# Down projection: chunks in the order 3, 3, 3, 3, 2, 2, and the low part of one activation in three formed by a negation and an adding DMA

## Chip, cores and metric

One core of one Trainium2 chip runs the whole program. The metric is the device time of one execution in microseconds, from the median of several runs. TensorE (PE) does the matmuls, VectorE (DVE), ScalarE (ACT) and GpSimd (POOL) the elementwise work, and SyncE (SP) issues nearly all DMAs.

## The reference, cut to what matters

One layer of a streaming encoder over 1152 tokens of width 1024: a norm, one wide input projection, three mixers (a convolution, an attention with forgetting, a gated recurrence), their gated sum through `w_o`, and a channel mixer. The change lies in the channel mixer and the final norm:

```
u = rms_norm(x, g2) @ w_up            # 1024 -> 4096
x = x + square(relu(u)) @ w_down      # 4096 -> 1024
y = rms_norm(x, final_g)
```

All is float32. The matmuls take pairs of a rounded high part (type fp32r) and a low part (value minus high part); one product is three matmuls: high by high, high by low, low by high.

## The kernel before, in words

**The channel mixer** (`back_half`, from L1393) works on transposed data: channels on 128 partitions, tokens along the free axis. Both matrix products are done by a fast 2 x 2 block scheme with 7 products in place of 8. Operands are combined before, and results after, by additions. The products are numbered 1 to 7 and run in the order of `SLOTS` (L41): 2, 6, 5, 7, then product 1 of the next run, then 4 and 3. So a run has seven slots. `go` (L1507) issues for each slot the matmuls (`mm`), then `hook(slot)`, then `after(p)`, which empties or adds the finished product. Three PSUM tiles X, Y and Z are shared by the products of a run; product 7 adds onto Y after product 6 was read from it.

**Up runs** (`URun`) are 16, u15 first and u14 last (tokens split over two runs for u15). Each leaves seven squared activations of 128x576, which SP writes to DRAM (`ad_d`).

**Down runs** (`DRun`) are grouped by chunks of the 16 inner blocks. `CHUNKS` (L38) is 2, 3, 3, 3, 3, 2. For a chunk of n blocks there are 7 n activations in SBUF and four runs, d(c)0 to d(c)3, one for each pair of output blocks; a product has 6 n matmuls of 288 columns. The last chunk has four runs with other shapes, where weights of two output blocks lie side by side (dA, dB) and the tokens are split in 384 and 192 columns (`LP`), so that the final norm of the first part can run beside the second. After each product `DRun.after` (L1816) adds it onto `xt` on DVE.

**Feeding the activations** (`feed`, L1778). `TF[0]` counts free tiles among 28 of one tag. For each free one, `feed` issues an SP load of the next activation of the list `todo` (chunk, product, block k) into the upper half of a tile (L1792). An activation may be split two hooks later, at most two in one hook: ACT casts it into the lower half (L1783), and DVE subtracts the cast from it in place (L1784, seen in the profile at its helper, L1369). Tiles come free as the last run of a chunk uses its products (`DRun.free`), and at the start as the last up run frees its inputs: the driver's `hook` (L1947) adds 2 in six of its slots, 2 in the slot before, and 14 more in d00 to d02, two at a time.

**Weights** (`Step`, L1409). A step loads four raw blocks two runs ahead, in slots 4, 5 and 6 (`load`), builds the other three by subtraction on DVE in slots 1 and 2 of the run before its own, and splits all seven into high and low parts with ACT and DVE (`prep`). In slot 1 of d20, for example, DVE must have the last raw block of d21. All engines run their instructions in program order, so a wait there holds back the additions onto `xt` behind it.

**The sums of squares** (`square`, L1867) of the final norm: ACT squares, then an addition into `ss`, whose engine is an argument with GpSimd as its default. Both calls (L1885, L1973) pass DVE. `final` multiplies `ss` by a column of ones on PE (`fst`, L1900) and spreads the result (`fsb`).

**hook_a** (L1739) runs in the first up run, over the first half of the tokens, beside the end of the second norm: slot 2 issues `N1.fin`, slot 4 `N1.spread`, which makes PE multiply by the diagonal `dg` into `rb` (L1627).

Of the kernel before, what the change touches and what calls it, by code (L numbers as in the profile page):

```python
# [12 lines left out]
ALU = mybir.AluOpType  # L13
# [21 lines left out]
PC = 576  # L35
HP = 288
NST = 16
CHUNKS = (2, 3, 3, 3, 3, 2)  # L38
LP = ((0, 384), (384, 192))
CTS = (0, 4, 1, 5, 2, 6, 3, 7)  # L40
SLOTS = (2, 6, 5, 7, 1, 4, 3)  # L41
# [72 lines left out]
def trunk(tc, I, O):  # L114
    nc = tc.nc
    PE, V, A, GP, SY = nc.tensor, nc.vector, nc.scalar, nc.gpsimd, nc.sync
# [9 lines left out]
    with pool("cn") as cn, pool("st") as st, pool("dr", DRAM) as dr, pool("tp") as tp, \  # L126
# [28 lines left out]
        def dram(name, shape, dt=F32):  # L155
            return dr.tile(shape, dt, name=name, tag=name)
# [18 lines left out]
        ad_d = dram("ad_d", [8, NST, P, PC])  # L175
# [61 lines left out]
        def T(name, dt=F32):  # L237
            return tp.tile([P, 1152], dt, tag="T", bufs=28, name=name)
# [93 lines left out]
        with pool("ps1", PSUM) as ps:  # L332
# [972 lines left out]
            while un[0] < NWIN:  # L1305
# [26 lines left out]
                elif name in ("f_c", "q_c", "o_c"):  # L1332
                    r = (i * 3 + ("f_c", "q_c", "o_c").index(name)) * P
# [3 lines left out]
                else:  # L1337
                    r = (("g_a", "g_b", "g_c").index(name) * 8 + i) * P
# [20 lines left out]
        def RT(name):  # L1359
            return qp.tile([P, 512], F32, tag="r", bufs=4, name=name)  # L1360
# [7 lines left out]
        def sub(eng, out, a, b):  # L1368
            eng.tensor_tensor(out=out, in0=a, in1=b, op=ALU.subtract)  # L1369

        def add(eng, out, a, b):
            eng.tensor_tensor(out=out, in0=a, in1=b, op=ALU.add)  # L1372
# [20 lines left out]
        def back_half(ps, ep, q2, on1):  # L1393
# [15 lines left out]
            class Step:  # L1409
# [5 lines left out]
                def raw(self, p):  # L1415
                    if p not in self.r:
                        if p in (1, 2) and self.early:
                            if p == 1:
                                self.rt = T(f"{self.name}rt")
                            self.r[p] = self.rt[:, (p - 1) * 512:p * 512]  # L1420
                        elif p in (4, 5, 6):
                            self.r[p] = q2.tile([P, 512], F32, tag="q2", bufs=3, name=f"{self.name}r{p}")
                        else:
                            self.r[p] = RT(f"{self.name}r{p}")
                    return self.r[p][:, :self.w]
# [81 lines left out]
            def go(run, nxt, hook):  # L1507
                for slot, p in enumerate(SLOTS):
                    r = nxt if p == 1 else run
                    if r is not None:  # L1510
                        r.mm(p)
                    hook(slot)
                    if r is not None:
                        r.after(p)
# [166 lines left out]
            for u in range(16):  # L1681
# [22 lines left out]
                if u >= 2:  # L1704
                    q, r = divmod(u - 2, 8)
# [25 lines left out]
            def more(n):  # L1731
                for _ in range(n):
                    if rest:
                        N1.split(*rest.pop(0))
                        if not rest:
                            N1.x.clear()
                            N1.e.clear()

            def hook_a(slot):  # L1739
                if slot == 0:  # L1740
                    st0.prep(5)
                elif slot == 1:
                    st0.prep(6)
                    N1.build(3, V)
                elif slot == 2:
                    N1.fin()
                    N1.split(6, 3)
                elif slot == 4:
                    N1.spread()
                if slot > 2:  # L1750
                    more(3)
# [8 lines left out]
                ustep(UO[1]).load(i)  # L1760

            NC = len(CHUNKS)
            TF = [0, 14]
            acts, todo, fly = {}, [], []
            xt = {}

            def x_back(j):
                for ch, hf in ((j, 0), (j + 4, 0), (j + 4, 1), (j, 1)):
                    t = xt[ch, hf] = E(f"xt{ch}{hf}")
                    SY.dma_start(t, xs_d[ch, hf])  # L1770

            K0 = [sum(CHUNKS[:c]) for c in range(NC)]
            for c in range(NC):
                for p in (1, 2, 6, 5, 7, 4, 3):
                    for k in range(CHUNKS[c]):
                        todo.append((c, p, k))

            def feed(most=2):  # L1778
                n = 0
                while fly and n < most and fly[0][1] <= 0:  # L1780
                    t = acts[fly.pop(0)[0]]
                    r = raw(t[:, PC:2 * PC])
                    A.copy(t[:, 0:PC], r)  # L1783
                    sub(V, t[:, PC:2 * PC], r, raw(t[:, 0:PC]))  # L1784
                    n += 1
                for f in fly:
                    f[1] -= 1
                while todo and TF[0] > 0:
                    c, p, k = key = todo.pop(0)
                    TF[0] -= 1  # L1790
                    t = acts[key] = T("a{}{}{}".format(*key), F32R)
                    SY.dma_start(raw(t[:, PC:2 * PC]), ad_d[p, K0[c] + k])  # L1792
                    fly.append([key, 2])

            FIN = {2: 0, 3: 1, 7: 2, 4: 3}
            done = []

            class DRun(Run):
# [11 lines left out]
                def free(self, p):  # L1810
                    if self.end:
                        for k in range(self.step.n):
                            del acts[self.c, p, k]
                            TF[0] += 1

# [23 lines left out]
            def dsrc(c, j, two=False):  # L1839
                cols = slice(K0[c] * P, (K0[c] + CHUNKS[c]) * P)  # L1840
                if two:
                    return lambda q: I["wdn"][j:j + 2, q].rearrange("j p c -> p j c")[:, :, cols]
                return lambda q: I["wdn"][j, q][:, cols]
# [3 lines left out]
            for c in range(NC - 1):  # L1847
                for j in range(4):
                    r = DRun(c, j, Step(f"d{c}{j}", dsrc(c, j), CHUNKS[c]))
                    r.end = j == 3  # L1850
                    runs.append(r)
            c = NC - 1
            sA = Step("dA", dsrc(c, 0, True), CHUNKS[c], True)
            sB = Step("dB", dsrc(c, 2, True), CHUNKS[c], True, wide=True)
            for j, step, pc in ((0, sA, 0), (2, sB, 0), (2, sB, 1), (0, sA, 1)):
                r = DRun(c, j, step, pc)
# [6 lines left out]
            def xv(pc, ch, hf):  # L1863
                b, n = LP[pc]
                return xt[ch, hf][:, b:b + n]

            def square(pc, ch, hf, eng=GP):  # L1867
                n = LP[pc][1]
                if ss[pc] is None:
                    ss[pc] = T(f"ss{pc}")[:, 0:2 * n]  # L1870
                t = ss[pc][:, hf * n:(hf + 1) * n]
                seen[pc] += 1
                if ch == (0, 2)[pc] + 4 * hf:
                    A.activation(t, xv(pc, ch, hf), AF.Square)
                    return
                q = T(f"fq{pc}{ch}{hf}")[:, 0:n]
                A.activation(q, xv(pc, ch, hf), AF.Square)
                add(eng, t, t, q)
# [64 lines left out]
            for i, r in enumerate(runs):  # L1943
                n = runs[i + 1] if i + 1 < len(runs) else None
                nn = runs[i + 2] if i + 2 < len(runs) else None

                def hook(slot):  # L1947
                    if r is last_u:
                        TF[0] += 2 if slot != 4 else 0
                    if n is last_u and slot == 4:  # L1950
                        TF[0] += 2
                    if n is last_u and slot == 0:
                        x_back(0)
                    if isinstance(r, DRun) and r.c == 0 and slot % 2 and r.j < 3 and TF[1] > 0:
                        TF[0] += 2
                        TF[1] -= 2
                    if rest:
                        more(1)
                    if isinstance(r, DRun) and r.c == 0 and r.j < 3 and slot == 1:
                        x_back(r.j + 1)  # L1960
                    feed()
                    if n is not None and n.step is not r.step:
                        n.step.prep(slot)
                    if nn is not None and nn.step is not n.step and nn.step.at == 0:
                        nn.step.load(slot)
                    if isinstance(r, DRun) and r.pc is not None:
                        for f in fins:
                            if 0 < slot < 5 or state[0] > 3:
                                next(f, None)
                                state[0] += 1  # L1970
                        k = 0
                        while done and k < 3 and (r is not runs[-4]) and not (r is runs[-1] and slot > 5):
                            square(*done.pop(0), V)  # L1973
                            k += 1
                        if seen[0] == 16 and not fins:
                            fins.append(final(0))

                go(r, n, hook)
                if r is last_u:
                    fs.clear()  # L1980
# [23 lines left out]
        with pool("ps3", PSUM) as ps:  # L2004
            back_half(ps, ep, q2, on1)
# [105 lines left out]
```

## Time and profile before

| | |
|---|---|
| median of 3 runs | 2084.15 us (2084.14 to 2086.68) |
| the profiled execution | 2087.83 us, its span 2086.1 us |
| granted TensorE clock, mean | 0.985 |
| PE busy | 2002.0 us, 96% of the span |
| DVE, ACT, POOL busy | 1458.8, 841.3, 533.5 us |
| DMA | 288.85 MB, mean 138 GB/s |

The span runs from the first to the last instruction of the profiled execution; times in rows are microseconds from its start. A busy share is an average over stages with different limits. The up runs end and the down runs begin at about 1672 us; POOL has nothing to do between 1315 and 2044 us.

### The profile page before, as it was taken

Reading aid. Unit: us, or ns where it says so; the run is one execution under the profiler, and the core shown is the slowest. Engines: PE = TensorE matmul, PEld = TensorE weight load, DVE = VectorE, ACT = ScalarE, POOL = GpSimd, SP = SyncE. Lnnn points to the kernel's source line nnn. Section 1 sums busy time; section 2 is a strip of 40 time slices with the busy share of each in tenths; the row PEclk is TensorE's granted clock in tenths of the full one; section 3 lists DMA queues with packets and bytes.
Section 4 is the critical chain, followed back from the end, with each engine's and each line's share of the span. In section 5 each row is a group of like instructions: output and inputs, shape, how many; then the busy total and the mean of one; then the engine's idle time right before and its main releaser. Section 6 shows DMA issues by size and latency. Waiting matters only on the chain. (4 is left out here: it accounts for less than half of the span.)

```text
span 2086.1 us, 37159 instructions
## 1 busy us (share of the span) xinstructions
PE 2002.0 (96%) x14345; PEld 1944.3 (93%) x14345; DVE 1458.8 (70%) x2458; ACT 841.3 (40%) x1581; POOL 533.5 (26%) x530
## 2 busy tenths in 40 slices
PE   8999999999999999999999999899999979999996
PEld 7899999999889898999999999899999979999996
DVE  6688888888854655657345777766666687877786
ACT  6433344434326353645311343433333443442432
POOL 4334544342531625335205444000000000000002
PEclk9999999999999999999999999999999999999997
DMA  5354443435444343343455254244344573552422
GB/s 174 126 161 128 132 146 99 123 99 137 153 148 148 116 131 117 123 131 99 151 210 202 68 184 142 89 147 154 121 150 151 194 249 122 165 165 80 132 81 91
DMA packets 202529, 288.85 MB, mean 138 GB/s; under 512 B 47112, under 2 KB 135368, under 8 KB 202352
## 3 DMA queue, kind: packets, MB, share of 16 engines
q1 hardware_dynamic: 202352, 286.47, 42.5%
q8 instruction: 113, 1.85, 0.4%
q14 instruction: 64, 0.52, 0.1%
HBM read 189.73 MB, written 96.67 MB: 137 GB/s over the span
## 5 line engine op out<-in xcount | busy, mean ns | idle before, releaser
L233 PE MATMUL pc<-hh,wh 128*128 128x384 f32 x1248 | 442.3, 354 | 8.8 <-ACT wh L204 5.2
L235 PE MATMUL pc<-hh,wl 128*128 128x384 f32 x1248 | 425.7, 341 | 2.0 <-DVE wl L216 2.0
L234 PE MATMUL pc<-hl,wh 128*128 128x384 f32 x1248 | 425.4, 341 | 1.6 <-DVE hl L386 1.6
L233 PEld LDWEIGHTS pc<-hh,wh 128*128 128x128 f32 x1248 | 237.8, 191 | 18.6 <-ACT wh L204 5.2
L234 PEld LDWEIGHTS pc<-hl,wh 128*128 128x128 f32 x1248 | 237.8, 191 | 5.5 <-DVE hl L386 4.0
L235 PEld LDWEIGHTS pc<-hh,wl 128*128 128x128 f32 x1248 | 237.2, 190 | 2.5 <-DVE wl L216 2.3
L1585 POOL TENSOR_TENSOR fr<-fr,cst 96x2 f32<-96x2 f32 (+1 forms) x3 | 3.0, 1005 | 739.7 <-DVE fr L1902 739.7
L549 DVE SCALAR_TENSOR_TENSOR y<-up,pv,y 128x768 f32<-128x768 f32 x120 | 131.5, 1095 | 0.2
L216 DVE TENSOR_TENSOR wl<-wr,wh 128x1024 fp32r<-128x1024 f32 (+1 forms) x71 | 91.2, 1286 | 56.1 <-ACT wh L215 55.6
L736 ACT ACTIVATE p<-s,m 128x128 f32<-128x128 f32 (+3 forms) x64 | 47.6, 744 | 177.6 <-DVE m L734 169.2
L552 POOL TENSOR_TENSOR y<-y,ud 128x256 f32<-128x256 f32 x120 | 108.3, 903 | 9.4
L551 POOL TENSOR_TENSOR ud<-up,pv 128x256 f32<-128x256 f32 x120 | 97.1, 809 | 7.4
L235 PE MATMUL y<-bh,wl 128*128 128x384 f32 x288 | 97.5, 339 | 0.0
L234 PE MATMUL y<-bl,wh 128*128 128x384 f32 x288 | 97.0, 337 | 0.0
L233 PE MATMUL y<-bh,wh 128*128 128x384 f32 x288 | 97.0, 337 | 0.0
L215 ACT CAST wh<-wr 128x1024 fp32r<-128x1024 f32 (+1 forms) x71 | 74.1, 1046 | 38.9 <-PE y L234 29.3
L233 PE MATMUL pt<-wh,hh 128*128 128x260 f32 (+1 forms) x288 | 84.2, 293 | 5.4 <-ACT vs L613 4.2
L320 POOL TENSOR_TENSOR gt<-gt,gt 128x384 f32<-128x384 f32 x45 | 53.5, 1189 | 126.3 <-DVE gt L319 115.7
L1369 DVE TENSOR_TENSOR a<-a 128x576 fp32r<-128x576 f32 x112 | 79.9, 751 | 6.2 <-ACT a L1783 6.2
L234 PE MATMUL pt<-wl,hh 128*128 128x260 f32 (+1 forms) x288 | 81.3, 282 | 0.9 <-DVE wl L216 0.9
L235 PE MATMUL pt<-wh,hl 128*128 128x260 f32 (+1 forms) x288 | 81.2, 282 | 0.0
L1783 ACT CAST a<-a 128x576 fp32r<-128x576 f32 x112 | 71.2, 673 | 24.3 <-DMA a<-ad_d 23.5
(832 smaller groups left out, 6136.0 us busy)
## 6 DMA issues: line engine op xcount, KB each, us to landing
wr<-in_wu SPq DMA_DIRECT2D x67, 512.0 KB
a<-ad_d SPq DMA_DIRECT2D x112, 288.0 KB
gt<-sg SPq DMA_DIRECT2D x24, 576.0 KB
wor<-in_wo SPq DMA_DIRECT2D x32, 256.0 KB
sg<-zgg_a SPq DMA_DIRECT2D x24, 192.0 KB
sg<-zgg_b SPq DMA_DIRECT2D x24, 192.0 KB
sg<-zgg_c SPq DMA_DIRECT2D x24, 192.0 KB
x<-in_xc SPq DMA_DIRECT2D x16, 288.0 KB
```

What stands on the lines that cost most here:

```text
L215: A.copy(h[:, :c], r[:, :c])
L216: V.tensor_tensor(out=l[:, :c], in0=r[:, :c], in1=h[:, :c].bitcast(F32), op=ALU.subtract)
L233: PE.matmul(out, lh, rh, start=start, stop=False, skip_group_check=again)
L234: PE.matmul(out, lh, rl, start=False, stop=False, skip_group_check=again)
L235: PE.matmul(out, ll, rh, start=False, stop=stop, skip_group_check=again)
L320: (V if n == 23 else GP).tensor_tensor(out=macc[ct][:, r], in0=macc[ct][:, r], in1=gt[:, r], op=ALU.add)
L549: V.scalar_tensor_tensor(out=y[:, :CD], in0=u[:, j:j + CD], scalar=w, in1=y[:, :CD], op0=ALU.mult, op1=ALU.add)
L551: GP.tensor_tensor(out=tm, in0=u[:, CD + j:NPR + j], in1=wp1, op=ALU.mult)
L552: GP.tensor_tensor(out=yp, in0=yp, in1=tm, op=ALU.add)
L736: A.activation(pr[:, 0:L], s[:, 0:L], AF.Exp, bias=m[:, 0:1], accum_out=m[:, 1:2])
L1369: eng.tensor_tensor(out=out, in0=a, in1=b, op=ALU.subtract)
L1783: A.copy(t[:, 0:PC], r)
```

## The change

Six edits. The chunks come in the order 3, 3, 3, 3, 2, 2. The counts by which `TF` is raised are fitted to a first chunk of 21 activations: 3 a slot around the last up run, and 7 more in d00 to d02, one at a time. In `feed` an activation with k % 3 == 1 no longer gets DVE's subtraction: ACT writes the negated cast over the raw values, and a DMA issued by GpSimd reads the raw values from DRAM once more and adds them onto it. `N1.spread` is issued in slot 5 of the first up run where it was slot 4. And the squares of the last chunk that are taken in a hook have their additions on GpSimd; those taken in `final` stay on DVE.

```diff
-CHUNKS = (2, 3, 3, 3, 3, 2)
+CHUNKS = (3, 3, 3, 3, 2, 2)
...
-                elif slot == 4:
+                elif slot == 5:
                     N1.spread()
...
-            TF = [0, 14]
+            TF = [0, 7]
...
-                    t = acts[fly.pop(0)[0]]
+                    c, p, k = key = fly.pop(0)[0]
+                    t = acts[key]
                     r = raw(t[:, PC:2 * PC])
                     A.copy(t[:, 0:PC], r)
-                    sub(V, t[:, PC:2 * PC], r, raw(t[:, 0:PC]))
+                    if k % 3 == 1:
+                        A.mul(t[:, PC:2 * PC], raw(t[:, 0:PC]), -1.0)
+                        GP.dma_start(r, ad_d[p, K0[c] + k], accum_op=ALU.add)
+                    else:
+                        sub(V, t[:, PC:2 * PC], r, raw(t[:, 0:PC]))
                     n += 1
...
                     if r is last_u:
-                        TF[0] += 2 if slot != 4 else 0
+                        TF[0] += 3 if slot != 4 else 0
                     if n is last_u and slot == 4:
-                        TF[0] += 2
+                        TF[0] += 3
...
                     if isinstance(r, DRun) and r.c == 0 and slot % 2 and r.j < 3 and TF[1] > 0:
-                        TF[0] += 2
-                        TF[1] -= 2
+                        TF[0] += 1
+                        TF[1] -= 1
...
-                            square(*done.pop(0), V)
+                            square(*done.pop(0))
```

## Rows read from the trace of the kernel before

**Rows 1.** Windows by stage: from and to (us), length, then busy time and count of PE, PEld (weight loads), DVE, ACT and POOL, the granted TensorE clock, the DMA engines' busy share and GB/s.
```profile
1677.00:1750.00 73.00, 60.68 (x426) 59.57 (x426) 66.45 (x120) 36.76 (x73) 0.00 (x0) 0.93 0.69 230
1750.00:1803.00 53.00, 53.00 (x403) 53.00 (x403) 37.38 (x64) 20.79 (x40) 0.00 (x0) 1.00 0.46 146
1803.00:1820.00 17.00, 14.56 (x108) 14.12 (x108) 15.60 (x27) 7.08 (x14) 0.00 (x0) 1.00 0.30 98
```

**Rows 2.** Waits of PE from 1560 to 2090 us, by the tile written and what ended the wait: total us, times, the longest.
```profile
PE d00None L233 <- DVE xt L1372: 7.1, 1, 7.1
...
PE d30None L233 <- DVE xt L1372: 2.7, 2, 1.8
PE d20None L233 <- DVE xt L1372: 2.4, 2, 1.5
PE d02None L233 <- DVE xt L1372: 2.2, 1, 2.2
PE d40None L233 <- DVE xt L1372: 1.8, 2, 0.9
...
PE d01None L233 <- DVE xt L1372: 1.2, 1, 1.2
PE d10None L233 <- DVE xt L1372: 1.1, 1, 1.1
PE d03None L233 <- DVE xt L1372: 0.7, 2, 0.4
```

**Rows 3.** Windows of 10 us at the entry of the down phase, columns as in rows 1.
```profile
1680.00:1690.00 10.00, 5.79 (x31) 5.82 (x32) 9.42 (x18) 4.66 (x10) 0.00 (x0) 0.66 0.99 339
...
1710.00:1720.00 10.00, 8.05 (x50) 8.08 (x51) 8.09 (x17) 3.94 (x9) 0.00 (x0) 0.83 0.66 215
```

**Rows 4.** Timeline at the entry of the down phase (start, length, engine, line, operation, out<-in; in brackets the idle time before it and what ended that): two of DVE's additions and a pair of activation splits between them, then PE.
```profile
1680.52 0.75 DVE L1372 TENSOR_TENSOR xt<-xt,d00None 128x576 f32<-128x576 f32 x1
1683.32 0.75 DVE L1372 TENSOR_TENSOR xt<-xt,d00None 128x576 f32<-128x576 f32 x1
1684.21 0.58 PE L233 MATMUL d00None<-a,d00h 128*128 128x288 f32 x1 [7.12 <-DVE xt L1372]
```

**Rows 5.** Timeline of DVE at the change to the third chunk (d20).
```profile
1805.56 1.42 DVE L1369 TENSOR_TENSOR a<-a 128x576 fp32r<-128x576 f32 x2
...
1808.46 0.56 DVE L1369 TENSOR_TENSOR d21r<-d21r,d21r 128x384 f32<-128x384 f32 x1 [1.01 <-DMA d21r<-in_wdn]
1808.93 0.75 DVE L1372 TENSOR_TENSOR xt<-xt,d20None 128x576 f32<-128x576 f32 x1
```

**Rows 6.** Timeline of SP's DMA issues in the same stretch (start of the first, time until the last is issued, how many).
```profile
1786.10 8.65 SPq L1792 DMA_DIRECT2D a<-ad_d  x12
...
1798.00 1.28 SPq L1792 DMA_DIRECT2D a<-ad_d  x3
...
1800.38 1.27 SPq L1792 DMA_DIRECT2D a<-ad_d  x3
1802.54 0.33 SPq L1432 DMA_DIRECT2D d21r<-in_wdn  x1
```

**Rows 7.** The DMA view of 1780 to 1830 us in 40 slices of 1.25 us: busy tenths of the 16 DMA engines, and GB/s.
```profile
DMA  9999337999999999997990140004000542004105
GB/s 284 310 294 325 108 112 168 334 265 354 278 337 345 375 399 351 354 310 175 364 357 28 37 125 0 0 21 136 0 7 0 143 111 61 13 0 113 44 0 143
```

**Rows 8.** A load on a quiet queue (256 KB, the last of dB): its issue by SP, and DVE's first use of it, with the wait for it.
```profile
2010.92 0.37 SPq L1432 DMA_DIRECT2D dBr<-in_wdn  x1
...
2014.40 0.69 DVE L1369 TENSOR_TENSOR dBr<-dBr,dBr 128x512 f32<-128x512 f32 x1 [0.71 <-DMA dBr<-in_wdn]
```

**Rows 9.** The activation splits of the whole down phase, by line and engine: count, total busy us and mean ns of one, and idle time before them.
```profile
L1369 DVE TENSOR_TENSOR a<-a 128x576 fp32r<-128x576 f32 x112 | 79.9, 751 | 6.2 <-ACT a L1783 6.2
L1783 ACT CAST a<-a 128x576 fp32r<-128x576 f32 x112 | 71.2, 673 | 24.3 <-DMA a<-ad_d 23.5
```

**Rows 10.** Timeline of ACT before d20: three of the casts of that chunk's activations.
```profile
1788.87 0.68 ACT L1783 CAST a<-a 128x576 fp32r<-128x576 f32 x1 [1.54 <-DMA a<-ad_d]
...
1791.62 1.36 ACT L1783 CAST a<-a 128x576 fp32r<-128x576 f32 x2
...
1798.94 1.25 ACT L1783 CAST a<-a 128x576 fp32r<-128x576 f32 x2
```

**Rows 11.** Timeline of PE in d20: the first matmul after its first wait.
```profile
1809.83 0.37 PE L233 MATMUL d20None<-a,d20h 128*128 128x288 f32 x1 [1.54 <-DVE xt L1372]
```

**Rows 12.** POOL's additions of the shape that the change moves to it (group of the whole span), and two rows of the timeline at 1300 us, a POOL addition and a DVE subtraction that overlap.
```profile
L320 POOL TENSOR_TENSOR gt<-gt,gt 128x384 f32<-128x384 f32 x45 | 53.5, 1189 | 126.3 <-DVE gt L319 115.7 <-issue 10.2 <-POOL gt L320 0.2
...
1299.50 1.88 POOL L1372 TENSOR_TENSOR sq<-sq,sq 128x576 f32<-128x576 f32 x1
...
1300.01 1.68 DVE L1369 TENSOR_TENSOR H<-x,H 128x288 fp32r<-128x288 f32 x1
```

**Rows 13.** Timeline in the last chunk: ACT's last squares of the first part of the tokens, and the matmuls that use the sum.
```profile
2040.41 0.99 ACT L1877 ACTIVATE fq<-xt 128x384 f32<-128x384 f32 x2 [1.35 <-DVE xt L1372]
...
2042.24 1.52 PE L1900 MATMUL fst<-on,ss 128*96 128x1 f32 x16
```

**Rows 14.** Timeline around the first up run: ACT's copy of product 7, PE's spread and its wait, and PE's next wait.
```profile
1313.67 0.39 ACT L1561 COPY u150e<-u 128x288 f32<-128x288 f32 x1
...
1315.60 2.26 PE L1627 MATMUL rb<-dg,on 96*128 96x288 f32 x4 [2.77 <-DVE dg L1586]
...
1326.39 0.61 PE L233 MATMUL u<-H,U15h 128*128 128x288 f32 x1 [3.10 <-ACT u L1505]
```

## The prediction
> **What bounds the kernel now.** I read the windows by stage first, to see where TensorE (PE) is not full. From 1750 to 1803 it is busy all the time, 403 matmuls in 53.00 us, 0.1315 us each; from 1677 to 1750 only 60.68 of 73 us, from 1803 to 1820 14.56 of 17 [rows 1]. So the last fifth of the kernel is bound by PE except at the entry of the down phase and at each change of chunk. At 0.1315 us a slot (one product of seven) takes 2.37 us in a chunk of 3 (18 matmuls), 1.58 in a chunk of 2, 3.16 in an up step.
>
> Then PE's waits: 7.1, 1.2, 2.2 and 0.7 us in d00 to d03, 11.2 in all; 1.1 for d10, 2.4 for d20, 2.7 for d30, 1.8 for d40, 8.0 in all [rows 2]. Each is a wait for `xt`, DVE's addition of a finished product, after which the next product may overwrite its PSUM tile. After two of them the clock fell: 31 matmuls took 5.79 us in 1680 to 1690 at a granted clock of 0.66, and 50 took 8.05 in 1710 to 1720 at 0.83 [rows 3]. That is 0.187 and 0.161 us each for 0.1315, or 1.7 and 1.5 us lost at the lower of the levels 1.2 and 2.4 GHz. The entry of down so costs 11.2 + 3.2 = 14.4 us, the changes of chunk 8.0.
>
> What holds DVE back differs. At the entry it is plain arrears: the first two additions of d00 run at 1680.52 and 1683.32, with activation splits between them, and PE goes on at 1684.21 [rows 4]. At d20 it is something else. Between two activation splits and the addition at 1808.93 lies a subtraction of weights that waited 1.01 us for a DMA, the load of d21's raw weights [rows 5]. SP issued that load at 1802.54, behind eighteen activation loads issued since 1786.10 [rows 6], and the DMA engines stand at nine tenths or more in almost every slice from 1788.75 to 1806.25, at 265 to 399 GB/s [rows 7]. On a quiet ring the same kind of load, 256 KB, went from issue at 2010.92 to its user at 2014.40, 3.48 us [rows 8]; here 192 KB took 5.92. **At a change of chunk DVE and the DMA queue are late together.**
>
> **The part that moves work to a DMA.** With k % 3 == 1, chunks of 3 give up 7 of 21 subtractions and chunks of 2 give up 7 of 14: 4 x 7 + 2 x 7 = 42 of 112. DVE loses 42 x 0.751 = 31.5 us [rows 9], hidden except at the waits above. ACT gains 42 negations at up to the cast's 0.673, 28 us, in an engine busy half the time at the entry and less elsewhere [rows 1]; each stands ahead of weight casts and seeds, so these come up to 0.7 us later. POOL, idle here, gets 42 DMA issues, each waiting for ACT's negation; behind them stand only other such issues, until the squares. PE waits for each landing instead of for DVE.
>
> Bounds for one addition by DMA: it can't be free of bytes, but could fall wholly into quiet stretches (0 us on the queue); the nearest row is the plain load of the same 288 KB, at 345 GB/s (between the figures of [rows 7]) 0.85 us of all 16 engines; it also fetches the tile it adds to, so up to two loads, 1.7 us. I take 0.85, the row that moves the same source bytes, and keep 0 and 1.7.
>
> At d20: feed takes at most two activations a hook. The casts that precede the additions of products 5, 7 and 4 start at about 1788.87, 1791.62 and 1798.94 [rows 10], so three additions enter the saturated stretch before the weight load is through: 3 x 0.85 = 2.55 us later. DVE's relief lets the load be issued perhaps 0.8 us earlier (its buffer is freed by a split in arrears), so it lands 1.7 us later. PE's first wait, 1.54 us of the 2.4 [rows 11], becomes 3.2; the second, 0.9, goes, since DVE has a third less to subtract. A wait of 2.2 lowered the clock [rows 3], so I add 1.5: 4.7 for 2.4. With d30 alike (2.7 before) and d10 now a change from 3 to 3 (1.1 before), that is +2.3, +2.0, +3.6. The fourth change now goes into a chunk of 2, whose slots are 0.8 us shorter: three slots on, PE asks 2.4 us sooner, with 0.4 back from smaller weights. First wait 0.9 + 1.7 + 2.0, clock 1.5, 6.1 for 1.8: +4.3. **Changes of chunk: +12** (0 on the queue: -3.5; two loads: +22).
>
> **Chunk order and TF at the entry.** Chunk 0 now wants 21 activations, loaded 3 a slot where 2 were, but 7 of its splits leave DVE, so DVE still subtracts 14 there. The last up step ends near 1673 (before 1672.2, plus one slot 0.8 us longer). Its chain of additions, squares and combinations stays on DVE. d00's second addition ended at 1684.1 [rows 4]; the weight operations ahead of it are half as wide again, some 1.2 us, so it ends at about 1685. The cast for product 7's block 1 stands in the hook just before it, so its negation ends near 1682.3, and the addition by DMA, 4 to 6 us later by [rows 8], at about 1687. Unhindered PE would start that product at 1673 + 3 x 2.37 = 1680.1. So some 6.5 us stay, with 1.7 of clock and 1 for product 3, whose addition is fed two slots before its use: 9 against 14.4. The waits of d01 to d03 go: in runs of 3 with few splits DVE was busy 37.38 of 53 us [rows 1], 11.7 in the 16.6 us of a run. **Entry: -5.4** (bounds -11 and +2). Runs of 2 now stand last, as d40 to d43, 11.1 us each; their weight operations are a third narrower than those in the 11.7 us, and after d40 they carry no activations, so: 0, at worst +1. The queue of SP carries the same 112 loads, seven more of them before d00.
>
> A sentence beside the sum: the Trainium skill, "DMA: Bandwidth & Descriptors", section on the anatomy of one DMA, gives 2.0 us plus the bytes at 436 GB/s for a DMA issued by GpSimd, 2.7 us for 288 KB. By it product 7 would wait for DVE alone, and the entry would be -7.4; [rows 8] with 3.48 us on a quiet ring speaks for more.
>
> **The squares.** In the last chunk the additions into `ss` go from DVE (under the 0.751 of a wider one [rows 9]) to POOL (1.19 for 128x384 [rows 12]). The last two squares for the first half leave ACT from 2040.41 [rows 13]; POOL ends them at 2040.9 + 2 x 1.19 = 2043.3, and the `fst` matmuls, which started at 2042.24, wait 1.1 us. POOL also slows DVE: a 128x288 subtraction took 1.68 us beside a POOL addition of 1.88 [rows 12], where one twice as wide takes 0.751 [rows 9]. DVE gets back some ten short additions. Together **+1** (-1.5 to +3).
>
> **The spread, one slot later.** `rb` waited 2.77 us for `dg`; product 4 can now run in that time, but only after ACT's copy at 1313.67. PE then waits 3.10 at 1326.39 for a seed behind the same DVE and ACT work [rows 14], so most of the gain turns into a longer wait there: **-0.5** (-1.5 to 0).
>
> Sum: 12 - 5.4 + 1 - 0.5 = **+7.1**. On the profiled execution of 2087.83 us that gives 2094.9; it stands 3.7 above the median of 2084.15, by which the forecast is **2091**.
>
> **Rivals.** *DVE's relief wins (faster).* Place: the weight load at each change of chunk. If less than about 0.45 us of an addition falls into the saturated stretch (three additions then cost 1.4 us, less 0.8 of earlier issue), the first waits stay under 2 us with no fall of the clock, and the sum turns to zero; below that it falls to -3.5 - 5.4 - 0.5 with the tail near 0, and to -14 with the better bound of the entry: 2070 to 2080, about 2075. For it: DVE was late as well, and there are idle slices at 1785 to 1788.75 [rows 7]. Against it: the 1.01 us wait for d21's weights shows the queue behind already. 0.31.
>
> *They cancel.* Additions cost about half a load: within 0.2% of 2084 (4.2 us, about what a measurement of this kernel can tell from no change). 0.19.
>
> *An addition costs two loads.* Each weight load comes 2.55 us later still, at four changes: +22 there, -2 at the entry, up to 2104. The Trainium skill says, in "Collectives: The Full Stack", section on the bandwidth ceiling, that an add in the DMA path needs two source reads and so runs at about half the rate; no run here shows it yet. For it from the rows: the tile must be fetched too. 0.2, against 0.3 for the forecast at one load.
>
> *The change doesn't do what it says.* The additions land after PE would have needed them everywhere, not only at the entry; then waits would stand at products of k = 1 in every chunk. The distance there is seven to eight slots, over 16 us, so I give it nothing of its own.
>
> **Numbers.** Slower 0.3 + 0.2 = 0.50, same 0.19, faster 0.31. The range reaches from the better bound, 2070, to two loads with the worse tail, 2106.
>
> **What would show it.** Right: the fresh profile has waits of d10, d20, d30 and d40 at 3 us or more, with DVE's weight subtractions waiting for `in_wdn` 2 us and longer just before; DMA slices full to about 3 us later; no waits in d01 to d03; 42 DMAs from POOL; DVE's `a` group at x70. Wrong: if the changes of chunk lose under 1.5 us each, additions by DMA are nearly free; if the waits end on the DMA's landing in `a`, latency and not the queue decides.

## Result, and the profile after

The changed kernel takes **2111.23 us** (median of 4 runs, 2108.56 to 2113.77) for 2084.39 before in the same session: ratio 1.0127, interval 1.0112 to 1.0142, so 26.8 us slower. Slower was the likeliest sign (0.5), but the time lies outside the range of 2070 to 2106: the size was wrong, by 20 us of 2091. The profiled execution took 2110.38 us, its span is 2108.6, 22.5 more than before.

The waits of PE (TensorE) in the changed kernel from 1560 us on (tile written, what ended the wait: total us, times, the longest), to be read beside [rows 2]:

```profile
PE d40None L233 <- DVE xt L1372: 11.6, 1, 11.6
PE d20None L233 <- DVE xt L1372: 7.9, 1, 7.9
PE d30None L233 <- DVE xt L1372: 6.9, 1, 6.9
PE d10None L233 <- DVE xt L1372: 6.8, 1, 6.8
PE d00None L234 <- DMA a<-ad_d: 4.8, 3, 2.3
...
PE d00None L233 <- DVE xt L1372: 2.5, 1, 2.5
```

The changes of chunk now wait 33.2 us, for 8.0 before; the entry, d00 to d03, 7.3 for 11.2. What DVE, which PE waits for, was itself waiting for (same stretch):

```profile
DVE d41r L1369 <- DMA d41r<-in_wdn: 7.5, 2, 3.9
DVE d21r L1369 <- DMA d21r<-in_wdn: 6.7, 2, 3.6
DVE d11r L1369 <- DMA d11r<-in_wdn: 6.6, 2, 5.2
DVE d31r L1369 <- DMA d31r<-in_wdn: 6.5, 2, 5.1
```

These are loads of raw weights (`in_wdn` holds them in DRAM): 27.3 us in all, for 2.8 before. The two largest before, the second of which is the 1.01 us of [rows 5]:

```profile
DVE d31r L1369 <- DMA d31r<-in_wdn: 1.3, 1, 1.3
DVE d21r L1369 <- DMA d21r<-in_wdn: 1.0, 1, 1.0
```

Windows of 10 us of the changed kernel (columns as in rows 1), the first three at the entry, the others behind the four changes, show the granted clock:

```profile
1670.00:1680.00 10.00, 7.73 (x49) 7.51 (x48) 8.46 (x14) 5.87 (x11) 0.90 (x2) 0.85 1.06 333
1680.00:1690.00 10.00, 4.96 (x27) 4.18 (x26) 8.10 (x15) 7.45 (x14) 2.37 (x3) 0.84 1.04 296
1690.00:1700.00 10.00, 10.00 (x64) 10.00 (x62) 5.04 (x9) 3.74 (x8) 1.03 (x2) 0.79 0.63 201
1760.00:1770.00 10.00, 5.79 (x27) 5.82 (x28) 6.28 (x11) 2.57 (x5) 0.87 (x1) 0.66 0.50 102
1840.00:1850.00 10.00, 8.70 (x55) 8.73 (x56) 8.71 (x15) 3.57 (x8) 0.00 (x0) 0.78 0.22 46
1910.00:1920.00 10.00, 3.51 (x16) 3.54 (x17) 4.90 (x10) 2.77 (x6) 0.87 (x1) 0.66 0.66 163
...
1990.00:2000.00 10.00, 6.81 (x35) 6.84 (x36) 6.46 (x13) 3.75 (x8) 1.74 (x2) 0.60 0.61 112
```

Busy time less 0.1315 us a matmul is what the lower clock took: 1.3 + 1.4 + 1.6 = 4.3 us at the entry, 2.2 + 1.5 + 1.4 + 2.2 = 7.3 at the changes. With the waits the changes cost 40.5 us for 8.0, **+32.5**; the entry 11.6 for 14.4, **-2.8**. The last chunk, from its first weight load to the end of the span, took 78.0 us for 84.0, **-6.0**. Together 23.7, for 22.5 us between the two spans. The changed kernel's execution is 3.0 us ahead at 1300 us already, where nothing is changed, so 1.8 us lie elsewhere. (That point is reached between 1295.3 and 1299.8 us in the thirteen profiles: differences of 2 or 3 us between two profiles are within such scatter.)

How late the weights are is best seen at d20. The span of the tile's weight loads (first and last start, us) in the changed kernel; then SP's issues; then DVE:

```profile
L233 PEld LDWEIGHTS d20None<-a,d20h x42: 187/188/330, 1818.8 to 1851.8; 128*128 128x128 f32 x42
```

```profile
1811.17 9.35 SPq L1797 DMA_DIRECT2D a<-ad_d  x12
1820.62 1.27 SPq L1432 DMA_DIRECT2D d21r<-in_wdn  x2
1823.07 1.28 SPq L1797 DMA_DIRECT2D a<-ad_d  x3
1824.96 0.33 SPq L1432 DMA_DIRECT2D d21r<-in_wdn  x1
1828.11 1.80 SPq L1797 DMA_DIRECT2D a<-ad_d  x3
1830.04 0.41 SPq L1432 DMA_DIRECT2D d21r<-in_wdn  x1
```

```profile
1835.77 0.56 DVE L1369 TENSOR_TENSOR d21r<-d21r,d21r 128x384 f32<-128x384 f32 x1 [3.08 <-DMA d21r<-in_wdn]
1839.93 0.56 DVE L1369 TENSOR_TENSOR d21r<-d21r,d21r 128x384 f32<-128x384 f32 x1 [3.61 <-DMA d21r<-in_wdn]
1840.41 0.74 DVE L1372 TENSOR_TENSOR xt<-xt,d20None 128x576 f32<-128x576 f32 x1
```

Counted from the first weight load of d20, the last raw block of d21 is issued at +11.2 us and used at +21.1. In the kernel before, d20 began at 1793.7, so the issue of [rows 6] was at +8.8 and the use of [rows 5] at +14.7: **issued 2.4 us later and used 6.4 us later**. Counted in the same way, the last raw block was issued 0.6, 2.4, 1.7 and 3.4 us later at d10, d20, d30 and d40, and used 6.6, 6.4, 5.1 and 7.8 us later. What SP waited for in that stretch, 1808 to 1832:

```profile
SPq L1797 <- PE d13None L235: 8.1, 10, 2.4
SPq L1432 <- DVE d21r L1369: 5.9, 1, 5.9
SPq L1797 <- DMA a<-ad_d: 3.4, 2, 2.8
...
SPq L1432 <- DMA a<-ad_d: 0.5, 1, 0.5
```

The rows that end on a DMA are new in this stretch: 3.9 us in which SP could not issue because an earlier load had not landed (had not told its completion). In the trace each of SP's DMAs waits for the semaphore of the one issued eight before it, so at most eight are under way: the load of 1828.11 was issued when the one of 1818.73 had landed, 9.3 us after its issue. Slow loads make SP late, not only the data.

And the price of an addition, in the table of DMA queues (packets, MB, share of 16 engines' span; q0 carries GpSimd's DMAs) and the issues (count, KB each, median us to landing) of the changed kernel:

```profile
q1 hardware_dynamic: 202352, 286.47, 41.8%
q0 software_dynamic: 6048, 12.39, 3.4%
...
a<-ad_d POOLq DMA_DIRECT2D x42, 288.0 KB, 6.9
```

0.034 x 2108.6 / 42 = **1.71 us of all 16 engines for one addition**.

### The profile page after: what moved, and what is told of

The parts are those of the page before. It is cut to its first block, busy times and chain, and to the rows that moved or that the text cites. A ratio compares the mean times of both kernels' runs of the same rounds, so it can differ in the third digit from the quotient of the medians.

```text
span 2108.6 us, 37261 instructions
## 1 busy us (share of the span) xinstructions
PE 2003.2 (95%) x14345; PEld 1947.2 (92%) x14345; DVE 1425.7 (68%) x2392; ACT 868.8 (41%) x1623; POOL 592.3 (28%) x596
## 3 DMA queue, kind: packets, MB, share of 16 engines
q0 software_dynamic: 6048, 12.39, 3.4%
## 4 chain that ended last, share of the span: by engine, by line
PE 51%; DMA 5%; issue 4%; POOL 4%; DVE 4%; ACT 2%; SPq 0%; DVEq 0%; POOLq 0%; ACTq 0%
PE u L233 5%; PE u L235 5%; PE u L234 5%; PE pc L233 3%; PE pc L235 3%; PE pc L234 3%; PE y L235 2%; PE y L234 2%; PE y L233 2%; POOL g L1083 1%; POOL g L1084 1%; PE wo L235 1%; PE wo L234 1%; PE wo L233 1%; DMA d41r<-in_wdn 1%
## 5 line engine op out<-in xcount | busy, mean ns | idle before, releaser
L1787 POOL DMA_DIRECT2D a<-ad_d x42 | 36.8, 877 | 649.4 <-ACT a L1786 525.0
L235 PE MATMUL wo<-mm,wol 128*128 128x288 f32 x256 | 76.2, 298 | 1.2 <-DVE wol L1369 1.2
```

The source lines that it names most:

```text
L235: PE.matmul(out, ll, rh, start=False, stop=stop, skip_group_check=again)
L1787: GP.dma_start(r, ad_d[p, K0[c] + k], accum_op=ALU.add)
```

## Experiments

Each comparison is with the kernel before, run on the same chip; "after" is the changed kernel.

**e1_sub**: after, all low parts by DVE again.
```diff
-                    if k % 3 == 1:
-                        A.mul(t[:, PC:2 * PC], raw(t[:, 0:PC]), -1.0)
-                        GP.dma_start(r, ad_d[p, K0[c] + k], accum_op=ALU.add)
-                    else:
-                        sub(V, t[:, PC:2 * PC], r, raw(t[:, 0:PC]))
+                    sub(V, t[:, PC:2 * PC], r, raw(t[:, 0:PC]))
```


> The changed kernel with DVE's subtraction back in place of the negation and the adding DMA; chunk order, TF, spread and squares stay changed. Theory A (the 42 adding DMAs overfill the DMA queue at each change of chunk, so the weight loads come late): the four changes lose 2 to 5 us each in place of 8 to 14, the waits of DVE for d11r, d21r, d31r and d41r fall from 6.5 us to under 2, SP no longer waits for its own earlier loads; about 2080 to 2088 us. Rival B (the chunk order, TF or the squares cost the time): the waits at d20, d30 and d40 stay near 7, 7 and 12 us and the time stays above 2100.

Measured 2077.47 us, ratio 0.9969 (0.9959 to 0.9979): **faster than both**. It lies below its expected range too. So the trick costs 34 us, and the rest of the change brings 7.

**e2_trick**: the kernel before with the trick alone (the lines that e1_sub takes out, put into the kernel before).

> The kernel before with the negation and the adding DMA alone (chunks 2, 3, 3, 3, 3, 2 and all else as before). Theory A: the changes d20, d30 and d40 lose 7 to 9 us each, with DVE waiting 5 us and more for d21r, d31r and d41r; d10, where only part of a chunk is fed at once, less; about 2100 to 2112 us. Rival B: it stays within 6 us of the kernel before, as DVE has 31 us less to do.

2121.56 us, 1.0184 (1.0167 to 1.0202), 38 us slower. It misses its expectation upwards. The entry, where this kernel has the old order and the old counts, suffers as well: PE waits 19.4 us in d00 to d03, for 11.2 before and 7.3 in the changed kernel. The largest wait of ACT, which casts the activations:
```profile
ACT a L1784 <- DMA a<-ad_d: 47.4, 18, 5.4
```
(before: 23.5 us for the same group [rows 9]); 22.1 of the 47.4 us lie ahead of d10.

**e3_nodma**: after without the addition; the low part of one activation in three stays the negated high part.
```diff
                         A.mul(t[:, PC:2 * PC], raw(t[:, 0:PC]), -1.0)
-                        GP.dma_start(r, ad_d[p, K0[c] + k], accum_op=ALU.add)
```


> The changed kernel without the adding DMA: the low part of one activation in three is only the negated high part, so that part of the computation is left out. It keeps DVE's relief and ACT's extra work and takes away what the DMA queue and POOL carry. Theory A: the waits at d10, d20, d30 and d40 fall to 0 to 2 us, at d40 to 2 to 4, the entry d00 under 5; about 2072 to 2080 us. Rival C (ACT's negations, queued ahead of weight casts and seeds, make DVE and PE late): the waits at the changes stay over 5 us each, above 2098.

2070.74 us, 0.9945 (0.9928 to 0.9962), slightly below what was expected. DVE's relief shows: 6.7 us below e1_sub, with ACT's negations in place. The two intervals overlap by a little, so that size is rough.

**e4_plain**: the same 288 KB from DRAM by the same queue, but written instead of added, so the low part is the raw value.
```diff
-                        GP.dma_start(r, ad_d[p, K0[c] + k], accum_op=ALU.add)
+                        GP.dma_start(r, ad_d[p, K0[c] + k])
```


> The changed kernel with the DMA from GpSimd as a plain load (it overwrites the negated part with the raw values, so that low part is wrong): same bytes from DRAM, same issue, no addition. It prices the addition against a load. If an addition costs two loads (1.71 us of 16 engines by the packet time of the queue, against about 0.9 for a load), the plain one shows 0.85 to 0.95 us each, weight loads wait about half as long, and the time lies halfway between the one without the DMA and the changed kernel, 2088 to 2100. Rival D (the fixed cost of a DMA issued by GpSimd and its completion decide, not its bytes): within 4 us of the changed kernel, 2107 to 2115.

2086.47 us, 1.0011 (1.0002 to 1.0021), below its expectation. Its queue of GpSimd's DMAs and their landing:
```profile
q0 software_dynamic: 3360, 12.39, 1.7%
...
a<-ad_d POOLq DMA_DIRECT2D x42, 288.0 KB, 4.8
```
0.017 x 2081.7 / 42 = 0.84 us (0.87 when its single packets are added up): **an addition takes the DMA engines twice as long as a load of the same bytes**, 144 packets each for 80. By the single packets an addition is moved in 128 pieces of 2304 bytes with a median of 195 ns, the load in 64 pieces of 4608 bytes with 178 ns; the rest are 16 packets of 4 bytes. In time the loads cost 86.5 - 70.7 = 16 us over e3_nodma, and making them additions 25 more: the second half of the engines' time costs more than the first. One reason is in the trace: SP waits 0.9 us for earlier activation loads to land here and 15.3 + 3.8 in the changed kernel (its rows for loads of activations and of weights), so here the last raw block is issued no later than in the kernel before (+8.7 at d20). At the four changes DVE waits for the weights 3.2 us in e3_nodma, 12.3 here and 27.3 after, and PE 4.2, 12.9 and 33.2.

**e8_wpool**: after, with the raw weights of the down runs issued by GpSimd, so that they don't stand behind SP's loads of activations; same bytes, same 42 additions.
```diff
-                        SY.dma_start(r.rearrange(...) if self.two else r, self.src(q))
+                        (GP if self.name[0] == "d" else SY).dma_start(r.rearrange(...) if self.two else r, self.src(q))
```


> The changed kernel with one edit: the raw weights of the down runs are loaded by GpSimd's queue in place of SP's, the same bytes, still with 42 adding DMAs. Theory: most of the cost of an addition is that SP holds eight DMAs in flight and issues a weight load only after the activation loads ahead of it have landed. Then the weight loads go out earlier, d10, d20, d30 and d40 wait 1 to 4 us each where they waited 7 to 12, and the time is 2085 to 2097. Rival: the 16 DMA engines are full until about 35 us after a chunk's change whoever issues, so the weights land as late: 2106 to 2114.

2088.63 us, 1.0021 (1.0009 to 1.0032): **some 22 of the 34 us are gone**, with the same 42 additions and the same loads (4.6 us over the kernel before on its chip, where the changed kernel was 26.8 over). PE's waits at the changes, from 1560 us on:
```profile
PE d40None L233 <- ACT a L1786: 7.3, 1, 7.3
...
PE d30None L233 <- DVE xt L1372: 1.9, 1, 1.9
...
PE d10None L233 <- DVE xt L1372: 1.7, 1, 1.7
...
PE d20None L233 <- DVE xt L1372: 1.5, 1, 1.5
```
12.4 us for 33.2; three of the four changes are in the expected 1 to 4 us. Its d20 begins at 1811.1. POOL issues the last raw block of d21, and DVE uses it, at
```profile
1819.88 0.56 POOL L1432 DMA_DIRECT2D d21r<-in_wdn  x1 [0.92 <-DVE d20l L1369]
```
```profile
1825.85 0.56 DVE L1369 TENSOR_TENSOR d21r<-d21r,d21r 128x384 f32<-128x384 f32 x1 [1.12 <-DMA d21r<-in_wdn]
```
that is +8.8 and +14.7 us, as in the kernel before, while the DMA engines stay at eight tenths and more until 1828.75, +17.6 us (its DMA view of 1795 to 1845 us, slices of 1.25):
```profile
DMA  0199528999999899999999999995599042400030
```
So what made the weights late at d10, d20 and d30 was that they shared SP's queue with the activation loads, not full engines as such. What is left is d40, where runs are a third shorter: there PE waits 7.3 us until 1968.55. The view puts the wait down to ACT's negation, which ends at 1968.46, but DVE's addition onto `xt` ends at 1968.40, and it stood behind a weight subtraction that waited:
```profile
1967.31 0.42 DVE L1369 TENSOR_TENSOR d41r<-d41r,d41r 128x256 f32<-128x256 f32 x1 [2.46 <-DMA d41r<-in_wdn]
1967.65 0.75 DVE L1372 TENSOR_TENSOR xt<-xt,d40None 128x576 f32<-128x576 f32 x1
```
So at d40 the weights are late on GpSimd's queue as well, with five additions issued between SP's first activation load and the last weight load where the other changes have three; which of the two, ACT or DVE, held PE can't be told from 0.06 us.

**e5_squares, e6_spread, e7_chunks**: the kernel before with one part of the change each.
```diff
# e5_squares
-                            square(*done.pop(0), V)
+                            square(*done.pop(0))
# e6_spread
-                elif slot == 4:
+                elif slot == 5:
                     N1.spread()
# e7_chunks
-CHUNKS = (2, 3, 3, 3, 3, 2)
+CHUNKS = (3, 3, 3, 3, 2, 2)
...
-            TF = [0, 14]
+            TF = [0, 7]
...
-                        TF[0] += 2 if slot != 4 else 0
+                        TF[0] += 3 if slot != 4 else 0
...
-                        TF[0] += 2
+                        TF[0] += 3
...
-                        TF[0] += 2
-                        TF[1] -= 2
+                        TF[0] += 1
+                        TF[1] -= 1
```


> The kernel before with one edit: the squares taken in a hook add on GpSimd. As forecast (+1 us, from the fst matmuls waiting 1.1 us): 2084 to 2087. Rival, from the fresh trace of the changed kernel, where fst waited only 0.81 us for POOL and the last chunk ran about 6 us shorter: DVE's relief in the last chunk shows, 2079 to 2083.

2082.03 us, 0.9987 (0.9978 to 0.9997): 2 to 3 us faster (by the interval 0.6 to 4.6), as the rival said. The last chunk takes 80.7 us for 84.0.

> The kernel before with one edit: the spread of the second norm in slot 5 of the first up run. By the trace of the changed kernel the waits there go from 2.77 + 3.10 to 0.24 + 5.49, a gain of 0.1 us: 2083.5 to 2084.8, no difference. Rival: the seed's wait was also due to other edits, and the whole 2.5 us come back: 2081.5 to 2082.5.

2084.84 us, 1.0003 (0.9994 to 1.0012): no difference.

> The kernel before with two edits only: chunks 3, 3, 3, 3, 2, 2 and the counts of free tiles fitted to them; squares and spread as before, the low parts all by DVE. The changed kernel with DVE's subtraction back took 2077.5, so if squares and spread are worth nothing this is 2077 to 2079 (the whole -7 is the order of the chunks). If the squares on GpSimd carry most of it: 2081 to 2084.

2081.97 us, 0.9986 (0.9976 to 0.9996), 2 to 3 us faster, the second case: the squares seem to carry about as much of e1_sub's 7 us as the order does, each no more than barely clear of noise. The three ratios multiply to 0.9976; e1_sub had 0.9969, and 0.9975 below.

**e9_sub_wpool, e10_mid, e11_sub_again**: can the trick pay once its harm is taken away? e9 has both edits of e1_sub and e8_wpool, e11 is e1_sub once more, and e10 is e8_wpool with
```diff
-                    if k % 3 == 1:
+                    if k % 3 == 1 and c in (1, 2, 3):
```


> No adding DMA (all low parts by DVE), the other five edits, and the weights of the down runs loaded by GpSimd's queue. If the weights no longer wait behind activation loads, the waits of DVE for them (0.6 and 0.2 us at d30 and d20 without this) and part of the 1.5 to 2.6 us of PE at the changes of chunk go: 2072 to 2077. If DVE's own arrears set those waits: 2076 to 2079, as without it (2077.5).

2082.28 us, 0.9987 (0.9978 to 0.9995), above both expectations. The last chunk took 83.6 us in its profile, for 79.9 in e11: the loss lies there, and why the weights' queue matters so late was not tested.

> The changed kernel with the weights on GpSimd's queue and the adding DMA only in chunks 1, 2 and 3 (21 in place of 42). The two places where the additions still cost with the weights moved, d00 (7.2 us of waits) and d40 (7.3), are those of chunks 0 and 4, so this should be 2072 to 2078, beside 2088.6 with all 42. Rival: the additions slow the plain loads of chunks 1 to 3 as well, by what is hidden so far: 2079 to 2086.

2080.01 us, 0.9976 (0.9967 to 0.9985), in the rival's range: the harm of the additions is gone, but no gain over the plain subtraction is left. Beside e9, which has the same queues and no additions, it is 2.3 us less, which the intervals don't separate.

> The changed kernel with DVE's subtraction in place of the adding DMA, once more and in more rounds, beside the two others: 2076 to 2079, ratio to before 0.996 to 0.998.

2079.11 us, 0.9975 (0.9965 to 0.9985). e10 and e11 can't be told apart; nothing tried with an adding DMA beats the plain subtraction.

## Why the prediction was wrong in size

**The changes of chunk (+12 forecast, +32.5 measured) hold the error.** Place and chain were right: the four changes, DVE's weight subtractions waiting for `in_wdn`, the additions onto `xt` behind them, PE behind those, then the clock. All the signs named for it appear: waits of 6.8 to 11.6 us, DVE's group of activation subtractions at x70, 42 DMAs of POOL, none of d01 to d03 among the waits. The DMA slices are full until 1837.5, 18.7 us after d20's first weight load, for 12.5 before: 6 us later, where 3 were forecast. The term was mis-sized in three steps.

- *"I take 0.85, the row that moves the same source bytes."* An addition took 1.71 us, the upper bound, and a load 0.84. The argument that the tile must be fetched too stood in the text and was given the smaller chance. That adds 2.6 us a change.
- *"Three additions enter the saturated stretch."* In the changed kernel POOL issued four between SP's first activation load and the last weight load. This is POOL's timeline there:
```profile
1817.23 0.88 POOL L1787 DMA_DIRECT2D a<-ad_d  x1 [7.18 <-ACT a L1786]
1820.08 0.87 POOL L1787 DMA_DIRECT2D a<-ad_d  x1 [1.97 <-DMA a<-ad_d]
1825.69 0.88 POOL L1787 DMA_DIRECT2D a<-ad_d  x1 [4.74 <-PE d13None L235]
1828.54 0.88 POOL L1787 DMA_DIRECT2D a<-ad_d  x1 [1.96 <-PE d20None L234]
```
4 x 1.71 = 6.8 us, near the 6.4 by which the weights came later; that the two are so close is in part luck, since a fifth was issued at 1832.83, before that load was used. At d10 and d30 it is four as well, at d40 six. In e4_plain and e8_wpool, where that load is issued in time, it is three at d10, d20 and d30: the count was right for a load that is not late.
- *"DVE's relief lets the load be issued perhaps 0.8 us earlier."* At d20 it was issued 2.4 us later, because SP waited for landings, and over the four changes 8.2 us later where 3.2 earlier were forecast. It is one reason why the bound of two loads (+22) did not hold the result: it doubled the price but kept three additions and an early issue.

The three steps can't be added up, since the late issue is itself a result of slow loads, and the further additions one of the late issue. What they make together can be: the forecast had the weights 1.7 us later at each change, and they were used 6.6, 6.4, 5.1 and 7.8 us later, 19 us more over the four. The term fell short by 20.5. Of these 26 us, 8 are late issue and 18 slow service; e8_wpool took both away at once, but for d40.

The lower clock, 1.5 us a change in the forecast, was 1.4 to 2.2.

**The rival of two loads named the price**, with 0.2 where the forecast had 0.3; its sum of 2104 was still 7 us short of the result. The Trainium skill, "Collectives: The Full Stack", section on the bandwidth ceiling, says of the reduce step of a collective that its add needs two source reads and so runs at about half the rate. The runs agree with the rate, 1.71 us for 0.84; that two reads are the reason they don't show.

**The entry (-5.4 forecast, -2.8 measured)** went as described: the waits of d01 to d03 left, d00 waits for the landing of additions, 7.3 us with DVE's part for 6.5 and 1 forecast, and the clock took 4.3 for 1.7. Without additions (e1_sub) d00's waits are 5.3. The Trainium skill, "DMA: Bandwidth & Descriptors", section on the anatomy of one DMA, gives 2.0 us plus bytes at 436 GB/s, an estimate of 2.7 us for 288 KB. Here a plain load by GpSimd (e4_plain) landed after a median of 4.8 us and at the least 2.9, which is near the estimate; an addition took 6.9, at the least 3.9. Most of them ran while the engines were nearly full.

**The squares (+1 forecast)** had the wrong sign: e5_squares is 2 to 3 us faster. The wait of `fst` for POOL came, 0.8 us for 1.1. But DVE's relief, taken as next to nothing, goes with a shorter last chunk: PE's waits for `xt` fall from 5.6 to 3.9 us. In the kernel before, the hooks' squares stand ahead of the additions onto `xt` on DVE, three at a time:
```profile
2027.98 1.88 DVE L1372 TENSOR_TENSOR ss<-ss,fq 128x384 f32<-128x384 f32 x3
2029.78 1.01 DVE L1372 TENSOR_TENSOR xt<-xt,d 128x384 f32<-128x384 f32 x2
2030.71 1.88 DVE L1372 TENSOR_TENSOR ss<-ss,fq 128x384 f32<-128x384 f32 x3
```
In e5_squares POOL has them, slower but out of the way:
```profile
2027.48 2.11 POOL L1372 TENSOR_TENSOR ss<-ss,fq 128x384 f32<-128x384 f32 x2
```
With the squares on GpSimd the last chunk took 77.7 to 80.7 us in eight of nine profiles (e9_sub_wpool: 83.6), and with them on DVE 83.0 to 84.2 in four. The granted clock differs there too, 0.77 for 0.70 on the mean of the 40 us that begin 46 ahead of the end (e5_squares, before); how much of the 3.3 us is clock was not separated.

**The spread (-0.5 forecast)**: PE's waits of 2.77 and 3.10 us [rows 14] became
```profile
1314.36 0.40 PE L233 MATMUL u<-H,U15h 128*128 128x288 f32 x1 [0.24 <-DVE u150e L1372]
1323.28 0.61 PE L233 MATMUL u<-H,U15h 128*128 128x288 f32 x1 [5.49 <-ACT u L1505]
```
as said: the gain turned into a longer wait, and e6_spread shows no difference.

**DVE's relief wins** was right in that DVE held PE up: with the additions left out the relief is worth some 6.7 us (e3_nodma against e1_sub). The additions took 40 (the changed kernel against e3_nodma), six times that.

## What to carry to other kernels

Before work is moved to a DMA, find the load that a late engine waits for, and count what will stand ahead of it: every DMA of the same queue, priced by the engine time that a profile shows for its kind and not by its bytes (here 1.71 us for 0.84), and the issues that wait for earlier landings. A queue that is just on time has no room. Here the cost beyond its slack grew faster than the engine time, 16 us and then 25, since late loads delayed the next issues and PE's clock fell after its waits. If the transfers must be there, try the urgent loads on another queue: that alone took some 22 us off here, and without the additions it brought nothing (e9_sub_wpool).

## What the runs showed of the hardware

- An adding DMA of 288 KB from DRAM into SBUF took 1.71 us of all 16 DMA engines and 144 packets, a plain one on the same queue 0.84 us and 80 packets; the profile counts the same 12.39 MB for 42 of either. The addition goes as 128 packets of 2304 bytes, median 195 ns, the load as 64 of 4608 bytes, 178 ns (each with 16 of 4 bytes). Median issue to landing 6.9 and 4.8 us, the shortest 3.9 and 2.9.
- Each DMA issued by SP waits for the landing of the one issued eight before it. With the additions SP waited 15.3 us for activation loads to land before it issued others, and 3.8 us before it issued weight loads; with plain loads in place of the additions 0.9 us and none.
- With the weights on GpSimd's queue and the activations on SP's, 192 KB were used 6.0 us after issue while the engines were full (1819.88 to 1825.85); behind the activations on SP's queue it was 9.9 us (1830.04 to 1839.93).
- POOL spent a median of 0.87 us on the issue of an addition, 0.55 on that of the plain load of the same bytes, and 0.54 on that of a 192 KB weight load.
